# A hybrid decoder block: two gate branches by seven products, earlier long-convolution projections, products issued in a fixed order

## The chip, the cores and the metric

The kernel runs on one core of a Trainium2 chip, in float32. The metric is device time in microseconds (us) of one execution; the number that counts is the median of the runs shown. The engines are TensorE (PE in the rows; PEld is its weight load), VectorE (DVE), ScalarE (ACT), GpSimd (POOL) and SyncE (SP, which issues nearly all weight loads).

## The reference, cut to what matters

512 tokens of width 1024 are normalised and projected; four mixers A to D make branch outputs y of width 256. Each is projected to width 1024 and multiplied by a sigmoid gate; the sum goes through an output projection and an MLP.

```python
D_MODEL, SEQ, N_MIXERS, MIX_W, D_FF = 1024, 512, 4, 256, 4096
xn = _rms(x, norm1_g[l])
# y_a: spatial gate, y_b: sparse attention, y_c: convolution of width 31 and layer norm, y_d: short convolution
z = ca * jax.nn.sigmoid(cb)
z = _causal_depthwise_conv(z, conf_conv_w[l]) + conf_conv_b[l]
y_c = jax.nn.silu(_layernorm(z, conf_ln_g[l], conf_ln_b[l]))
ys = jnp.stack([y_a, y_b, y_c, y_d], axis=2)
proj = jnp.einsum('bsnc,ncd->bsnd', ys, w_branch[l])
gates = jax.nn.sigmoid(jnp.einsum('bsd,de->bse', xn, w_gate[l]) + b_gate[l]).reshape(B, S, N_MIXERS, D)
mixed = jnp.sum(gates * proj, axis=2)
x = x + jnp.einsum('bsd,de->bse', mixed, w_out[l])
hn = _rms(x, norm2_g[l])
hid = jnp.square(jax.nn.relu(jnp.einsum('bsd,df->bsf', hn, w_mlp1[l])))
x = x + jnp.einsum('bsf,fd->bsd', hid, w_mlp2[l])
```

## The kernel before, in words

**Numbers as pairs.** Every float32 operand of a large matmul is held as a hi part and a lo part in a matmul format. ACT makes hi by a cast, DVE makes lo by a subtraction (`split`, L73 to L75). A product of two such operands takes three matmuls: hi with hi, hi with lo, lo with hi (`mm3`, L78 to L81). The transposed xn is XH and XL.

**Stages, in order of PE.** Projections and attention preparation; the gates of branch A (n=0); projections cb, ca, sh, sC, sB of mixers C and D; the gates of branch D (n=3), then B (n=1), then C (n=2); the output projection wo; MLP1 and MLP2 in four rounds (fq). Attention and the long convolution are Tasks: small steps that `tick` puts between the matmuls of the stage that runs. The long convolution's 60 multiply-add steps on DVE (L673) can begin once ca is projected.

**Gates** (`gate_branch`, i the place in that order, n the branch). Output columns go in eight tiles of 128; each is 24 matmuls of 128x512 (8 row blocks by three) into a PSUM tile gt, and a tanh on ACT (L868) into an SBUF tile g. After two gates the piece wb of the branch weights is projected: two tiles pj of 6 matmuls of 128x512. DVE forms (g+1)·pj (L882, L884) and the sum over branches is kept in MIX: written by DVE for the first branch, added to by POOL for the second and third, by DVE for the last (L885), which also splits it into MH and ML for wo.

**Weights** come as a list of pieces in the order of use. `take` hands out the next one; `get` makes two more ahead (ACT cast, DVE subtraction) and starts the loads of two beyond. The hi and lo tiles rotate through 3 buffers each, so the cast for a piece waits until PE has read the piece three before it for the last time.

**Seven products.** From the second part of MLP1 on, a block of 256 output columns by 512 tokens over 1024 rows is cut into quadrants and computed by seven half-size products instead of eight. `Group.make` forms the weight sums on DVE (L189 to L195); the token sums T4 to T7 are made once. `product` issues 24 matmuls of 128x256 per product (L1076 hi·hi, L1079 hi·lo, L1082 lo·hi) into one half of a PSUM tile xz of two banks, product 2 into a tile y of its own. Later products go on adding to what stands in xz; between them ACT copies or DVE adds intermediate values into R, the result in SBUF: after 1 an ACT copy (L1093), after 6 one (L1095), after 7 one (L1099), after 2, 7 and 3 a DVE add (L1089). Product 5 starts in the bank beside 1's, but in the same tile. Names: p27 is product 7 of group 2.

**Order.** The program is emitted in the order above, but a scheduler may reorder PE's work: in MLP1 before the change it put matmuls of other products between two that depend on each other. All dependencies are kept by tile: whoever writes xz waits for the last reader of xz.

Of the kernel before, what the change touches and what calls it, by code (L numbers as in the profile page):

```python
# [8 lines left out]
F32 = mybir.dt.float32  # L9
# [7 lines left out]
P = 128  # L17
# [20 lines left out]
def block_kernel(ctx: ExitStack, tc: tile.TileContext, x, w_in, w_branch, w_gate, w_out,  # L38
# [52 lines left out]
    def piece(name, srcs, nk, alloc=None):  # L91
# [62 lines left out]
    gate_pieces(0)  # L154
    for nm, c in (("cb", C_CB), ("ca", C_CA), ("sh", C_SH), ("sC", C_SC), ("sB", C_SB)):
        win(nm, [(c, 256)], False)
    gate_pieces(3)
    gate_pieces(1)
    gate_pieces(2)
    for q in range(2):  # L160
        for k in range(4):
            piece(f"wo{q}{k}", [w_out[k * 256 : (k + 1) * 256, q * 512 : (q + 1) * 512]], 2,
                  lambda tag, nm: wop[0].tile([P, 1024], F32R, tag=tag, name=f"{tag}_{nm}"))
    NQ = 8
    hps = []
    groups = {}

    class Group:


        def __init__(self, g):
            self.g, self.raw = g, {}

        def load(self):
            if self.raw or not hps:
                return
            for i, j in ((0, 0), (1, 0), (1, 1), (0, 1)):
                r = hps[0].tile([P, 4, 256], F32, tag="rawg", name=f"rawg_{self.g}{i}{j}", bufs=6)
                c0 = (4 * self.g + 2 * i) * P
                nc.sync.dma_start(r, w_mlp1[j * 512 : (j + 1) * 512, c0 : c0 + 256].rearrange("(k p) c -> p k c", p=P))  # L180
                self.raw[i, j] = r

        def make(self, n):
# [3 lines left out]
            if n == 5:  # L187
                self.s = hps[0].tile([P, 4, 256], F32, tag="sg", name=f"sg_{self.g}", bufs=1)
# [8 lines left out]
            v = [walloc(tag, f"p{self.g}{n}")[:, :1024].rearrange("p (k c) -> p k c", k=4) for tag in ("hi", "lo")]  # L197
            split(src, v[0], v[1])
            return v

    seqs = []
    for fq in range(4):
# [14 lines left out]
        for u in seq:  # L217
            if u[0] == "F":
                piece(f"m1_{u[1]}", [w_mlp1[:, u[1] * P : (u[1] + 1) * P]], 8)
            elif u[0] == "P":  # L220
                g = groups.setdefault(u[1], Group(u[1]))
                pieces.append((g.load, lambda g=g, n=u[2]: g.make(n)))
# [627 lines left out]

    MIX = big.tile([P, KT, S], F32, tag="mix", name="MIX")
    MH, ML = [], []

    def gate_branch(i, n, Yf):
        last = i == 3
        Y = None
        for c4 in range(4):
            gts = []
            for j in range(2):
# [7 lines left out]
                gt = br.tile([P, S], F32, tag="gt", name=f"g{n}_{dt}", bufs=4)  # L867
# [29 lines left out]
    gate_branch(0, 0, ya)  # L897

# [8 lines left out]
    def ca_done(j, acc):  # L907
        ca = br.tile([P, S], F32, tag="gt", name=f"ca_{j}", bufs=4)
# [7 lines left out]
    tct = Task(c_tail(), tcv)  # L916

# [37 lines left out]
    np_ = att_stack.enter_context(tc.tile_pool(name="np", bufs=1, side="right", reuse_waits="tile"))  # L955
# [5 lines left out]
    gate_branch(3, 2, yc)  # L961
    assert not tasks

# [97 lines left out]
    xz, yy = {}, {}  # L1061

    def product(g, n, w):
        hi, lo = w
        th, tl = TS[n]
        if n == 1:
            xz[g] = ps2(f"xz_{g}")
            R[g, 0], R[g, 1] = rtile(f"R{g}0"), rtile(f"R{g}1")
        if n == 2:
            yy[g] = ps(f"y_{g}")  # L1070
        acc = yy[g] if n == 2 else xz[g][:, int(n in (3, 5)), :]
        acc = acc.rearrange("p (i c) -> p i c", i=2)
        for p in range(2):
            sl = slice(p * P, (p + 1) * P)
            for kk in range(4):
                nc.tensor.matmul(acc[:, p, :], hi[:, kk, sl], th[:, kk, :],  # L1076
                                 start=kk == 0 and p == 0 and n in (1, 2, 5), stop=False,
                                 skip_group_check=True)
                nc.tensor.matmul(acc[:, p, :], hi[:, kk, sl], tl[:, kk, :], start=False, stop=False,  # L1079
# [133 lines left out]
```

## Time and profile before

| | |
|---|---|
| median of 3 runs | 826.03 us (825.67 to 826.28) |
| the profiled execution | 825.89 us, of which the span is 824.2 us and 1.7 us lie around it |
| PE busy | 806.9 us, 98% of the span |
| DVE busy | 494.3 us, 60% |
| ACT busy | 356.7 us, 43% |
| POOL busy | 86.6 us, 11% |
[...]

The profile prints busy times by engine and by groups of equal instructions, and the idle time before each with the instruction that ended it. Matmuls are pipelined: the printed duration of one (0.39 us for 128x512) is longer than the distance to the next, so the cost of a matmul is read from the distance of two starts.

### The profile page before, as it was taken

How to read it: one execution, taken by the hardware profiler on the slowest of the kernel's cores; microseconds unless marked ns; L12 is line 12 of the kernel's file. 1: busy time of each engine (PE TensorE's matmuls, PEld its weight loads, DVE VectorE, ACT ScalarE, POOL GpSimd, SP SyncE). 2: the span in 40 equal slices, each digit the busy share in tenths (PEclk: the TensorE clock that was granted, in tenths of full speed). 3: DMA queues.
4: the chain of work that ended last, by engine and by line, in shares of the span. 5: the costliest groups of instructions: out<-in, count | busy, mean ns of one | idle time of the engine just before them, and what ended most of it. 6: DMA issues, size and time to landing. Idle time of an engine off the chain costs nothing.

```text
span 824.2 us, 11467 instructions
## 1 busy us (share of the span) xinstructions
PE 806.9 (98%) x4577; PEld 685.9 (83%) x4577; DVE 494.3 (60%) x812; ACT 356.7 (43%) x577; POOL 86.6 (11%) x82
## 2 busy tenths in 40 slices
PE   7999999999999999999999999999999999999998
PEld 5989787777887888888888888889988898889987
DVE  5977764446999635743635758436753575447551
ACT  6645534443433323523524565513662266325630
POOL 6010011122443112120000000000000000000000
PEclk9999999999999999999999999999999999999999
DMA  9272222321222333333454134421442134310121
GB/s 307 82 203 58 74 81 65 103 78 51 65 64 65 115 91 101 90 98 94 143 177 140 39 124 157 128 78 52 119 138 101 30 99 153 104 52 26 52 103 52
DMA packets 94648, 81.41 MB, mean 99 GB/s; under 512 B 3874, under 2 KB 81986, under 8 KB 94595
## 3 DMA queue, kind: packets, MB, share of 16 engines
q1 hardware_dynamic: 93330, 76.61, 30.8%
q10 hardware_dynamic: 720, 2.62, 0.9%
q0 software_dynamic: 544, 1.45, 0.6%
q8 instruction: 36, 0.59, 0.3%
q14 instruction: 18, 0.14, 0.0%
HBM read 78.05 MB, written 2.10 MB: 97 GB/s over the span
## 4 chain that ended last, share of the span: by engine, by line
PE 94%; DVE 2%; ACT 2%; DMA 1%; issue 1%; SPq 1%; DVEq 0%; ACTq 0%
PE gt L79 7%; PE gt L81 7%; PE gt L80 7%; PE o L79 7%; PE o L80 7%; PE o L81 7%; PE xz L1076 5%; PE xz L1082 5%; PE xz L1079 5%; PE pj L79 2%; PE pj L81 2%; PE pj L80 2%; PE wo L81 2%; PE wo L79 2%; PE wo L80 2%; PE pv L605 2%
## 5 line engine op out<-in xcount | busy, mean ns | idle before, releaser
L79 PE MATMUL gt<-XH,hi_wg 128*128 128x512 f32 x256 | 101.8, 398 | 0.0
L81 PE MATMUL gt<-XH,lo_wg 128*128 128x512 f32 x256 | 101.2, 395 | 0.0
L80 PE MATMUL gt<-XL,hi_wg 128*128 128x512 f32 x256 | 100.7, 393 | 0.0
L80 PE MATMUL o<-lo_m,hd 128*128 128x512 f32 x248 | 97.9, 395 | 0.0
L79 PE MATMUL o<-hi_m,hd 128*128 128x512 f32 x248 | 94.5, 395 | 0.0
L81 PE MATMUL o<-hi_m,hd 128*128 128x512 f32 x248 | 93.4, 394 | 0.0
L75 DVE TENSOR_TENSOR lo_wg<-raw_wg,hi_wg 128x1024 fp32r<-128x1024 f32 x32 | 39.1, 1223 | 61.9 <-ACT hi_wg L74 61.8
L75 DVE TENSOR_TENSOR lo_p<-rawg,hi_p 128x1024 fp32r<-128x1024 f32 x35 | 42.8, 1223 | 45.5 <-ACT hi_p L74 45.5
L74 ACT CAST hi_wg<-raw_wg 128x1024 fp32r<-128x1024 f32 x32 | 33.5, 1047 | 82.9 <-PE gt L80 57.9
L74 ACT CAST hi_m<-raw_m 128x1024 fp32r<-128x1024 f32 x36 | 37.7, 1048 | 72.5 <-PE o L81 45.3
L75 DVE TENSOR_TENSOR lo_m<-raw_m,hi_m 128x1024 fp32r<-128x1024 f32 x36 | 44.1, 1224 | 39.0 <-ACT hi_m L74 39.0
L1076 PE MATMUL xz<-T,hi_p 128*128 128x256 f32 x224 | 56.2, 284 | 4.2 <-ACT R L1093 2.2
L583 POOL TENSOR_SCALAR p<-p,c 128x128 f32<-128x128 f32 (+3 forms) x32 | 42.8, 1349 | 157.4 <-DVE c L581 145.5
L81 PEld LDWEIGHTS gt<-XH,lo_wg 128*128 128x128 f32 x256 | 48.1, 188 | 11.8 <-issue 0.5
L74 ACT CAST hi_p<-rawg 128x1024 fp32r<-128x1024 f32 x35 | 36.7, 1049 | 47.1 <-PE xz L1079 23.6
L80 PEld LDWEIGHTS gt<-XL,hi_wg 128*128 128x128 f32 x256 | 48.2, 188 | 10.7
L79 PEld LDWEIGHTS gt<-XH,hi_wg 128*128 128x128 f32 x256 | 48.1, 188 | 10.7 <-issue 0.3
L81 PEld LDWEIGHTS o<-hi_m,hd 128*128 128x128 f32 x248 | 46.6, 188 | 10.9
L1079 PE MATMUL xz<-T,hi_p 128*128 128x256 f32 x224 | 55.6, 281 | 0.0
L80 PEld LDWEIGHTS o<-lo_m,hd 128*128 128x128 f32 x248 | 46.5, 188 | 10.5
L79 PEld LDWEIGHTS o<-hi_m,hd 128*128 128x128 f32 x248 | 46.5, 188 | 10.5
L1076 PEld LDWEIGHTS xz<-T,hi_p 128*128 128x128 f32 x224 | 42.1, 188 | 5.8 <-ACT R L1093 3.1
(405 smaller groups left out, 1870.5 us busy)
## 6 DMA issues: line engine op xcount, KB each, us to landing
raw_m<-in_w_mlp_dram SPq DMA_DIRECT2D x36, 512.0 KB, 3.4
raw_wg<-in_w_gate_dram SPq DMA_DIRECT2D x32, 512.0 KB, 4.0
rawg<-in_w_mlp_dram SPq DMA_DIRECT2D x28, 512.0 KB, 3.7
raw_wb<-in_w_branch_dram SPq DMA_DIRECT2D x16, 256.0 KB, 2.8
raw_wo<-in_w_out_dram SPq DMA_DIRECT2D x8, 512.0 KB, 4.3
x<-in_x_dram SPq DMA_DIRECT2D x4, 512.0 KB, 6.9
raw_kv<-in_w_in_dram SPq DMA_DIRECT2D x4, 512.0 KB, 4.3
w<-in_cmp_w_dram SPq DMA_DIRECT2D x4, 512.0 KB, 6.1
```

Source lines behind the costliest of these rows:

```text
L74: i = nc.scalar.copy(hi, src)
L75: (eng or nc.vector).tensor_tensor(out=lo, in0=src, in1=f32(hi), op=ALU.subtract)
L79: nc.tensor.matmul(dst, l[0], r[0], start=start, stop=False)
L80: nc.tensor.matmul(dst, l[0], r[1], start=False, stop=False)
L81: nc.tensor.matmul(dst, l[1], r[0], start=False, stop=stop)
L583: nc.gpsimd.tensor_scalar_mul(p_[:, b, :w], p_[:, b, :w], c2[:, b : b + 1])
L605: nc.tensor.matmul(dst[i], V[:, k, b, g * HD : (g + 1) * HD], pts[h - 1 + i][:, b, k * P : (k + 1) * P], start=False, stop=b == 1 and k == t)
L1076: nc.tensor.matmul(acc[:, p, :], hi[:, kk, sl], th[:, kk, :], start=kk == 0 and p == 0 and n in (1, 2, 5), stop=False, skip_group_check=True)
L1079: nc.tensor.matmul(acc[:, p, :], hi[:, kk, sl], tl[:, kk, :], start=False, stop=False, skip_group_check=True)
L1082: nc.tensor.matmul(acc[:, p, :], lo[:, kk, sl], th[:, kk, :], start=False, stop=kk == 3 and p == 1 and n in (2, 3, 4), skip_group_check=True)
```

## The change

It does three things. The gates of branches B (n=1) and C (n=2), third and fourth in order, are computed by groups of seven products like MLP1's: two groups per branch, each for 512 gate columns. The hi and lo token sums that this needs (TX4 to TX7) are formed on DVE and ACT from XH and XL after attention has ended, into space that attention's tiles held; TX5 overwrites a quadrant of XH and XL. The pieces cb and ca, and so the long convolution, come before the gates of branch A instead of after them. And each product's matmuls are issued behind the last matmul of the product before (`tc.issue_after`), in MLP1 too.

```diff
+    def seven(g, n, w, TS):
...
+        with tc.issue_after(prod[0].ins) if prod else nullcontext():
...
+        prod[:] = [e]
...
+    def gate_group_pieces(n, first):
+        seq = []
+        for h in range(2):
+            if first and h == 0:
+                o = [1, 2, 5, 6, "J0", 7, "J2", 4, 3]
+            else:
+                o = [1, 5, 6, 2, 7, "J0", 4, 3, "J2"]
...
+    for nm, c in (("cb", C_CB), ("ca", C_CA)):
+        win(nm, [(c, 256)], False)
+    gate_pieces(0)
+    for nm, c in (("sh", C_SH), ("sC", C_SC), ("sB", C_SB)):
+        win(nm, [(c, 256)], False)
+    gate_pieces(3)
+    gate_group_pieces(1, True)
+    gate_group_pieces(2, False)
...
+                acc = seven((n, h), v, w, TX)
...
+                if v == 1:
+                    nc.scalar.copy(r1[:, :, a], acc)
+                elif v == 6:
+                    nc.scalar.copy(r1[:, :, b], acc)
+                elif v == 2:
+                    nc.vector.tensor_tensor(out=r1[:, :, a], in0=r1[:, :, a], in1=acc, op=ALU.add)
+                elif v == 7:
+                    nc.scalar.copy(r2[:, :, b], acc)
+                    nc.vector.tensor_tensor(out=r2[:, :, b], in0=r2[:, :, b], in1=z, op=ALU.add)
+                    for p in range(2):
+                        gate(r2[:, p, b], r2[:, p, b], 4 * h + 2 + p)
+                elif v == 4:
+                    for p in range(2):
+                        gate(r2[:, p, a], acc[:, p, :], 4 * h + 2 + p)
+                elif v == 3:
+                    nc.vector.tensor_tensor(out=r1[:, :, b], in0=r1[:, :, b], in1=z, op=ALU.add)
...
-    gate_branch(2, 1, yb)
+    yb()
     att_stack.close()
...
+    def xdiff(name, a, b):
+        t, u = graw(f"{name}a"), graw(f"{name}b")
+        for d, k in ((t, 0), (u, 1)):
+            nc.vector.tensor_tensor(out=d, in0=f32(a[k]), in1=f32(b[k]), op=ALU.subtract)
+        nc.vector.tensor_tensor(out=t, in0=t, in1=u, op=ALU.add)
+        return t
...
+    t1 = xdiff("tx1", xq[0, 1], xq[0, 0])
+    t3 = xdiff("tx3", xq[1, 1], xq[0, 1])
+    split(t3, *TX[7])
+    t2 = xminus("tx2", xq[1, 1], t1)
+    split(t2, *TX[6])
+    t4_ = xminus("tx4", xq[1, 0], t2)
+    split(t4_, *TX[4])
+    TX[5] = xq[0, 1]
+    split(t1, *TX[5])
+    gate_groups(2, 1, yb)
...
-    gate_branch(3, 2, yc)
+    gate_groups(3, 2, yc)
```

J0 and J2 stand for the two projections of branch weights in a group (pieces wb). In the rows below pg104 is the weight piece of product 4 of branch 1's group 0, pg11... that of its group 1, pm23 that of product 3 of MLP1's group 2; a number at the end of a name is that of a tile. A row with x4 stands for four matmuls.

PE, branch B from product 7 of the first group on. Before, two gates into PSUM tiles of their own, and their projections:

```order
L79 MATMUL gt1_2_3178<-XH_130,hi_wg110_3086 128x512
...
L81 MATMUL gt1_3_3211<-XH_130,lo_wg111_3149 128x512
L79 MATMUL pj1_2_3244<-YB0_140,hi_wb11_3172 128x512
...
L81 MATMUL pj1_3_3253<-YB0_140,lo_wb11_3173 128x512
```

Now:

```order
L916 MATMUL xz_g10_3120<-TX70_3064,lo_pg107_3209 128x256 x4
L81 MATMUL pj1_2_3300<-YB0_140,lo_wb11_3238 128x512
...
L81 MATMUL pj1_3_3307<-YB0_140,lo_wb11_3238 128x512
L911 MATMUL xz_g10_3120<-TX40_3068,hi_pg104_3255 128x256
...
L916 MATMUL xz_g10_3120<-TX40_3068,lo_pg104_3256 128x256 x4
L911 MATMUL xz_g10_3120<-XH_130,hi_pg103_3296 128x256
```

Between products 7 and 4 of this group stand eight matmuls of pj, and product 3 follows product 4 at once.

DVE, the end of the token sums ahead of the first group's product 6 (tx are the sums, sg and rawg the weight sums, crs and csq the layer norm of mixer C, g3 and pj3 the last gates of branch D). Before, at the same projections pj3_6 and pj3_7, DVE has only weight pieces and gates:

```order
L75 TENSOR_TENSOR lo_wg101_3014<-raw_wg101_2947,hi_wg101_3013 128x1024
L884 SCALAR_TENSOR_TENSOR g3_6_2978<-g3_6_2978,pj3_6_3019 128x512
L884 SCALAR_TENSOR_TENSOR g3_7_3011<-g3_7_3011,pj3_7_3028 128x512
L75 TENSOR_TENSOR lo_wb10_3038<-raw_wb10_2984,hi_wb10_3037 128x512
L694 TENSOR_TENSOR cv_2244<-cv_2244,cmu_3068 128x512 x2
```

Now:

```order
L75 TENSOR_TENSOR XL_131<-tx1a_3070,XH_130 128x4x256
L183 TENSOR_TENSOR rawg_g1010_3096<-rawg_g1000_3094,rawg_g1010_3096 128x1024
...
L1025 SCALAR_TENSOR_TENSOR g3_6_3011<-g3_6_3011,pj3_6_3039 128x512
L1025 SCALAR_TENSOR_TENSOR g3_6_3011<-g3_6_3011,pj3_7_3048 128x512
L75 TENSOR_TENSOR TX41_3069<-tx4_3087,TX40_3068 128x1024
L75 TENSOR_TENSOR lo_pg105_3113<-sg_g10_3110,hi_pg105_3112 128x1024
...
L185 TENSOR_TENSOR rawg_g1001_3100<-rawg_g1001_3100,sg_g10_3110 128x1024
L75 TENSOR_TENSOR lo_pg106_3148<-sg_g10_3110,hi_pg106_3147 128x1024
```

Fifteen DVE instructions now stand from the write of XL to the lo part of product 6's weights, the two included.

PE, second round of MLP1. Before, product 5 of the next group and a part of its product 6 stand between products 4 and 3:

```order
L1082 MATMUL xz_3_5146<-HH_3842,lo_p31_5078 128x256 x4
L1076 MATMUL xz_2_4983<-T40_4445,hi_p24_5109 128x256
...
L1082 MATMUL xz_2_4983<-T40_4445,lo_p24_5110 128x256 x4
L1076 MATMUL xz_3_5146<-T50_4430,hi_p35_5176 128x256
...
L1076 MATMUL xz_3_5146<-T60_4440,hi_p36_5207 128x256
L1076 MATMUL xz_2_4983<-HH_3842,hi_p23_5142 128x256
```

Now product 3 follows product 4:

```order
L916 MATMUL xz_m3_5545<-HH_4239,lo_pm31_5475 128x256 x4
L911 MATMUL xz_m2_5382<-T40_4842,hi_pm24_5506 128x256
...
L916 MATMUL xz_m2_5382<-T40_4842,lo_pm24_5507 128x256 x4
L911 MATMUL xz_m2_5382<-HH_4239,hi_pm23_5539 128x256
...
L916 MATMUL xz_m2_5382<-HH_4239,lo_pm23_5540 128x256 x4
L911 MATMUL xz_m3_5545<-T50_4827,hi_pm35_5573 128x256
```

The same holds in the third and fourth rounds.

## Rows read from the trace of the kernel before

**Rows 1.** The page: busy time by engine, and the granted clock in 40 slices.

```profile
PE 806.9 (98%) x4577; PEld 685.9 (83%) x4577; DVE 494.3 (60%) x812; ACT 356.7 (43%) x577; POOL 86.6 (11%) x82
...
PEclk9999999999999999999999999999999999999999
```

**Rows 2.** Waits of PE: who waited, for whom, us in total, times, longest.

```profile
PE xz L1076 <- ACT R L1093: 2.2, 4, 0.7
PE xz L1076 <- DVE R L1089: 1.9, 3, 0.6
PE xz L1076 <- ACT hi_p L74: 1.6, 1, 1.6
PE xz L1076 <- ACT R L1053: 1.2, 1, 1.2
PE y L1082 <- DVE lo_p L75: 0.8, 1, 0.8
```

**Rows 3.** Timeline of PE, one gate: start, duration, instruction, [idle before <-releaser].

```profile
354.76 0.40 PE L79 MATMUL gt<-XH,hi_wg 128*128 128x512 f32 x1
...
362.88 0.39 PE L81 MATMUL gt<-XH,lo_wg 128*128 128x512 f32 x1
```

**Rows 4.** Timeline of PE, product 1 and the start of product 5 in MLP1.

```profile
562.05 0.28 PE L1076 MATMUL xz<-HH,hi_p 128*128 128x256 f32 x1
...
563.47 0.29 PE L1076 MATMUL xz<-HH,hi_p 128*128 128x256 f32 x1
...
564.42 0.63 PE L1082 MATMUL xz<-HH,lo_p 128*128 128x256 f32 x4
565.73 0.38 PE L1076 MATMUL xz<-T,hi_p 128*128 128x256 f32 x1 [0.67 <-ACT R L1093]
565.96 0.28 PE L1079 MATMUL xz<-T,hi_p 128*128 128x256 f32 x1
```

**Rows 5.** Timeline of PE, ACT and DVE, product 7 to product 4 in MLP1.

```profile
577.67 0.63 PE L1082 MATMUL xz<-T,lo_p 128*128 128x256 f32 x4
577.87 1.05 ACT L74 CAST hi_p<-rawg 128x1024 fp32r<-128x1024 f32 x1 [0.56 <-PE xz L1079]
...
578.83 0.58 ACT L1099 COPY R<-xz 128x512 f32<-128x512 f32 x1
...
580.10 0.68 DVE L1089 TENSOR_TENSOR R<-R,xz 128x512 f32<-128x512 f32 x1
...
580.83 0.38 PE L1076 MATMUL xz<-T,hi_p 128*128 128x256 f32 x1 [0.65 <-DVE R L1089]
```

**Rows 6.** Timeline of PE, the first MLP1 group: product 3 behind product 4.

```profile
525.76 0.38 PE L1076 MATMUL xz<-HH,hi_p 128*128 128x256 f32 x1 [1.17 <-ACT R L1053]
```

**Rows 7.** Timeline, the first MLP1 group: product 2's wait, behind half of product 5.

```profile
498.91 0.38 PE L1076 MATMUL xz<-T,hi_p 128*128 128x256 f32 x1 [0.22 <-ACT R L1093]
...
499.84 0.27 PE L1079 MATMUL xz<-T,hi_p 128*128 128x256 f32 x1
...
500.88 0.74 PE L1082 MATMUL y<-HH,lo_p 128*128 128x256 f32 x4 [0.77 <-DVE lo_p L75]
```

**Rows 8.** Groups of DVE and POOL instructions: busy us, mean ns | idle before.

```profile
L673 DVE SCALAR_TENSOR_TENSOR cv<-Z,sm,cv 128x512 f32<-128x512 f32 x60 | 45.6, 790 | 0.4
...
L75 DVE TENSOR_TENSOR lo_wg<-raw_wg,hi_wg 128x1024 fp32r<-128x1024 f32 x32 | 39.1, 1223 | 61.9 <-ACT hi_wg L74 61.8
...
L884 DVE SCALAR_TENSOR_TENSOR g<-g,pj 128x512 f32<-128x512 f32 x24 | 16.3, 683 | 7.7 <-PE pj L81 7.5
```

**Rows 9.** Timeline of DVE around two adds of POOL to MIX.

```profile
264.95 0.68 DVE L884 SCALAR_TENSOR_TENSOR g<-g,pj 128x512 f32<-128x512 f32 x1
265.55 1.19 DVE L75 TENSOR_TENSOR lo_wb<-raw_wb,hi_wb 128x512 fp32r<-128x512 f32 x1
266.65 1.78 DVE L673 SCALAR_TENSOR_TENSOR cv<-Z,sm,cv 128x512 f32<-128x512 f32 x1
```

**Rows 10.** Timeline of PE and ACT: a cast for the next branch weights, waiting.

```profile
351.51 0.39 PE L80 MATMUL pj<-YB,hi_wb 128*128 128x512 f32 x1
351.94 0.62 ACT L74 CAST hi_wb<-raw_wb 128x512 fp32r<-128x512 f32 x1 [1.09 <-PE pj L80]
```

**Rows 11.** Busy us (instructions) by stretch of PE, PEld, DVE, ACT, POOL; clock, DMA share, GB/s.

```profile
205.00:240.00 35.00, 35.00 (x175) 28.10 (x174) 35.00 (x54) 14.21 (x26) 13.89 (x7) 1.00 0.22 62
240.00:268.00 28.00, 28.00 (x153) 22.21 (x152) 26.85 (x39) 9.76 (x17) 11.66 (x6) 1.00 0.22 66
```

More of the change, by code (lines that the diff above doesn't have):

```diff
@@ L849, in block_kernel @@
         proj_T("gu", gu_done, j)
+    xz, yy, prod = {}, {}, []
+    def seven(g, n, w, TS):
+        hi, lo = w
+        th, tl = TS[n]
+        if n == 1:
+            xz[g] = ps2(f"xz_{groups[g].name}")
+        if n == 2:
+            yy[g] = ps(f"y_{groups[g].name}")
+        acc = yy[g] if n == 2 else xz[g][:, int(n in (3, 5)), :]
+        acc = acc.rearrange("p (i c) -> p i c", i=2)
+        with tc.issue_after(prod[0].ins) if prod else nullcontext():
+            for p in range(2):
+                sl = slice(p * P, (p + 1) * P)
+                for kk in range(4):
+                    nc.tensor.matmul(acc[:, p, :], hi[:, kk, sl], th[:, kk, :],
+                                     start=kk == 0 and p == 0 and n in (1, 2, 5), stop=False, skip_group_check=True)
+                    nc.tensor.matmul(acc[:, p, :], hi[:, kk, sl], tl[:, kk, :], start=False, stop=False,
+                                     skip_group_check=True)
+                for kk in range(4):
+                    e = nc.tensor.matmul(acc[:, p, :], lo[:, kk, sl], th[:, kk, :], start=False,
+                                         stop=kk == 3 and p == 1 and n in (2, 3, 4), skip_group_check=True)
+        prod[:] = [e]
+        for _ in range(2):
+            tick()
+        return acc
@@ L851, in block_kernel, with branch_mm, mix_in @@
     MIX = big.tile([P, KT, S], F32, tag="mix", name="MIX")
     MH, ML = [], []
+    def branch_mm(n, c4, Y):
+        w, = take()
+        r = []
+        for j in range(2):
+            dt = 2 * c4 + j
+            pp = ps(f"pj{n}_{dt}")
+            sl = slice(j * P, (j + 1) * P)
+            for c in range(2):
+                mm3(pp, (w[0][:, c, sl], w[1][:, c, sl]), (Y[0][:, c, :], Y[1][:, c, :]), c == 0, c == 1)
+            r.append((dt, pp))
+        return r
+    def mix_in(i, dt, gt, pp):
+        mx = MIX[:, dt, :]
+        last = i == 3
+        nc.vector.scalar_tensor_tensor(out=gt, in0=gt, scalar=1.0, in1=pp, op0=ALU.add, op1=ALU.mult)
+        (nc.vector if last else nc.gpsimd).tensor_tensor(out=mx, in0=mx, in1=gt, op=ALU.add)
+        if last:
+            if dt % 2 == 0:
+                MH.append(t4(f"MH{dt}", [P, 2, S], F32R))
+                ML.append(t4(f"ML{dt}", [P, 2, S], F32R))
+            split(mx, MH[-1][:, dt % 2, :], ML[-1][:, dt % 2, :])
```

138 lines of the change are left out of this document (91 added, 47 removed).

## Prediction

> **What bounds the kernel now.** I read the busy times by engine first: PE is busy 98% of the span at the full granted clock, DVE 60%, ACT 43% [rows 1]. So the kernel is worth what PE's instruction stream is worth, plus PE's waits. The list of PE's waits comes second: behind the start, all that is longer than half a microsecond lies in MLP1's seven-product part, about 7.7 us together [rows 2]; in the stages that the change rebuilds PE waits for nothing. Third, the timelines give prices. A change can therefore win only by taking columns off PE, and loses by every wait that it brings into a stage that has none.
>
> **The price of a matmul.** Of a gate, 36 starts lie between 354.76 and 362.88: 8.12 / 35 = 0.232 us per 128x512 matmul [rows 3]. Of a product, 12 matmuls lie between 562.05 and 563.47: 0.1183 us per 128x256, so 24 of them cost 2.84 us [rows 4].
>
> **The price of a wait.** At product 5 behind product 1 the trace prints 0.67 us of idle time. The last matmul of product 1 has its slot until 564.42 + 4 x 0.118 = 564.90, so PE lost 0.83 up to 565.73, and the first matmul after it takes 0.23 instead of 0.12 [rows 4]. One such wait costs 0.94 us. The printed 1.17 of product 3 directly behind product 4 [rows 6] costs 0.50 more, 1.44.
>
> **Columns saved.** Each group replaces four gates, 96 x 0.232 = 22.27 us, by seven products, 168 x 0.1183 = 19.87 us. Four groups: 9.6 us less PE work. The branch projections stay the same.
>
> **Waits inside the groups.** The same dependencies by tile that give the waits of MLP1 come with the products. I take them by pair, with 0.94 as the lower price and about 1.9 as the upper one (0.94 and one ACT cast of 1.05 [rows 5] that stands ahead of the copy in ACT's queue).
>
> 1 to 5: in three groups product 5 directly follows product 1, and waits for ACT's copy out of the same xz tile. In groups 1 of B and 0 of C a weight cast and, in the first, a tanh stand ahead of that copy on ACT; I take 1.4, 1.6 and 0.94: 3.9 (2.8 to 5.7). The first group puts product 2 between, which covers it.
>
> 7 to 4: product 4 waits for the DVE add that follows ACT's copy. In MLP1 product 7's last slot ended at 577.67 + 4 x 0.118 = 578.14, the add at 580.78, and product 4 started at 580.83: 2.69 us behind [rows 5]. The groups of the second order have more than 2.8 us of other matmuls there, so nothing is lost. The first group has only eight pj matmuls, 8 x 0.232 = 1.86: 0.83 + 0.11 = 0.94 lost, and DVE has a backlog there; I take 1.5 (0.9 to 1.9).
>
> 4 to 3: product 3 waits for ACT's reading of 4's result. The second order puts eight pj matmuls between, so none; the first group has none between, and two tanh instructions and a cast have to pass on ACT: nearest is the row with 1.17; I take 1.75 (0.9 to 1.9).
>
> Second branch weights J2: with three buffers the hi cast of a group's second wb waits until PE has read the first one's last hi part, and PE's next instruction but one wants it. In the row, the cast starts 0.43 after the start of that matmul and takes 0.62 [rows 10]; PE has two matmuls, 0.46, to do until then, so about 0.6 + 0.11 = 0.7 is lost, in three groups: 2.1 (0 if the casts are released earlier, to 2.4).
>
> **First group's token sums.** They begin when attention's tiles are free. The place that decides is XL's quadrant: its ACT cast (1.05, and 0.3 of release) waits for branch D's last gate, then DVE has to pass fifteen instructions to the lo part of product 6: eight of 1024 columns and seven of 512. By the durations of 1.22 and 0.68 and the overlap of 0.08 between neighbours [rows 8, 9] that is 8 x 1.14 + 7 x 0.60 = 13.3 us, in all 14.7. PE has meanwhile 12 + 4 projection matmuls, three products and 8 matmuls of the fourth: 16 x 0.232 + 80 x 0.1183 = 13.2 us. So PE waits 1.5 us (0, if the casts come earlier, to 2.3, if all earlier sums are late too).
>
> What the row says of POOL beside this: DVE's instructions with both inputs in SBUF took 1.19 and 1.78 us while POOL added to MIX, against some 0.68 and 0.79 for their size [rows 8], and the one with an input in PSUM kept its 0.68 [rows 9]. [...]
>
> Sum of waits in the groups: 3.9 + 1.5 + 1.75 + 2.1 + 1.5 = 10.8 us (4.6 to 14.2). Against 9.6 saved: **+1.2 us** (-5.0 to +4.6).
>
> **Long convolution moved ahead of branch A's gates.** It adds no instruction. Its 60 steps of about 0.67 to 0.79 us [rows 8] leave a stretch where DVE is full: 35.0 of 35 us and 26.9 of 28, PE waiting for nothing [rows 11]. In the new place, from ca's projection to A's last one, I add up 72 us of DVE work against 280 matmuls of 128x512 and the small ones of attention, some 75 us of PE. DVE is nearly full there, in small steps between the lo parts of the weights, and those are made two pieces ahead. The rows show that PE gets through such a stretch, so I cost it at nothing; without that cover it costs what DVE exceeds PE by. The eight matmuls of its layer norm only move from branch B to branch D.
>
> **Fixed order in MLP1.** First group: half of product 5 ran while product 2's lo part was late, and PE still waited 0.77 [rows 7]. Without that filler (8 matmuls, 0.95 us) the wait is 0.95 longer. Rounds two to four: the wait of product 4 for DVE (0.65 each, three times [rows 2]; 0.9 with the restart) goes, since all 24 matmuls of the next product 1 (2.84) now stand before it and the add needs 2.69. In its place product 3 directly follows product 4 and waits for ACT: 0.94 each. Net zero; the three waits of 1 to 5 stay. In all **+0.95 us** (-1.8, if ACT is early at 4 to 3, to +2.5, if it costs 1.44 each).
>
> **Forecast.** 825.89 + 1.2 + 0.95 = 828.0 in the profiled execution; that run lies 0.14 below the median, so 828.2 us. About 0.2% is what a measurement of this kernel tells from no change: the bounds are 824.4 and 827.7, so this is slower, by little.
>
> **Rivals.** *The waits are as small as in MLP1's own groups.* There a round of 14 products shows two waits, 0.67 and 0.65 [rows 2], so 0.94 per group. Four groups: 3.8, no wait for sums or branch weights. Then 9.6 - 3.8 = 5.8 saved, MLP1 gives 0.95 back: 821.2 us, faster. For it: same code, same engines, and the copies' queues on ACT are only half full (43%). Against it: MLP1 runs two groups into each other, so that one covers the other's pairs, and the gates don't. It decides where the waits in the groups sum to less than 7.0 us. *The waits eat the saving exactly*: a wait sum of 7.0 to 10.3, 824.4 to 827.7, middle 826. *DVE's backlog reaches PE.* Where conv, softmax steps and lo parts share DVE, POOL's work stretches two-input steps by 0.5 to 1.1 us [rows 9]; ten such steps more than I counted turn 72 us of DVE into 80 against 75 of PE, and 5 us of wait come on top of 828: about 833. For it speaks DVE at 100% [rows 11], against it that PE didn't wait there before. [...] *That the change doesn't do what it says* I give nothing: the order shows seven products per group and no mixing.
>
> **How the numbers follow.** Forecast, slower by 0.3 to 5 us: 0.36; DVE backlog, above that: 0.11; even: 0.24; small waits, faster: 0.29. The range reaches from the small-waits case, 821.2, to near the backlog case, 832.5; beyond it I leave some 0.1 at either end. The forecast's own range is 827.7 to 831. Chances: faster 0.29, within 0.2% 0.24, slower 0.47.
>
> **What the changed profile should show.** PE busy time less by about 9 us, but waits of 11 us more. In PE's list of waits: three of product 5 for the ACT copy in the groups, one each of products 4 and 3 in the first group, of product 6 for its weights or sums, three of pj for hi_wb; in MLP1 three of product 3 for ACT and none of product 4 for DVE; product 2's at 1.7 us. From ca to the end of A's gates no wait. Between the first product of B and the first matmul of wo 1.2 us more than before between B's first gate and wo (488 x 0.232 = 113 us). The prediction is wrong if this list is short (the waits were overrated) or if waits for lo_wg appear beside the convolution.

## The result: slower by 1.45%, and the profile after

The changed kernel takes 838.05 us in the median of 4 runs (836.38 to 839.07); the kernel before took 825.85 us beside it (825.52 to 826.28). The ratio is 1.0145, with a 95% interval of 1.0128 to 1.0163. The sign was forecast, but the size was not: 828.2 us was forecast, with a range up to 832.5.

The profiled execution has a span of 837.3 us, 13.1 more than before. First come the lines of the profile's page that answer to [rows 1]:

```profile
PE 804.8 (96%) x4865; PEld 699.1 (83%) x4865; DVE 554.2 (66%) x866; ACT 379.8 (45%) x613; POOL 88.0 (11%) x82
...
PE   7999999999999998898999998999999999999998
```

Compared with 806.9, PE's busy time falls by 2.1 us, where the prediction wanted about 9 and the four groups hold 9.6 us less work by starts; DVE has 60 us more. The stages, by the starts of their first matmuls:

| stage | before, us | after, us | difference |
|---|---|---|---|
| up to the first product of B (before: first gate) | 308.35 | 310.13 | +1.8 |
| B and C, up to wo | 113.2 | 121.0 | +7.8 |
| wo | 45.7 | 45.7 | 0 |
| MLP1, first tiles | 26.7 | 27.5 | +0.8 |
| MLP1's products and MLP2, to PE's last product of MLP1 | 293.2 | 295.9 | +2.8 |

The 1.8 us of the first row are the eight layer norm matmuls (8 x 0.232) that moved there from the second one. So B and C lost 9.6 us where 1.2 were forecast, and the seven-product part of MLP1 lost 2.8 where 0.95 was forecast. The 0.8 us in MLP1's first tiles were not forecast at all: PE waits 1.09 us there for the lo part of the normalised tokens, HL, instead of 0.20. In every profile with branch C in groups this wait is 0.66 to 1.61 us, and in those without groups it is 0.20; why HL comes later was not followed.

PE's waits of the whole kernel (who waited, for whom, us in total, times, longest), which answer to [rows 2]:

```profile
PE xz_g L911 <- ACT g L970: 5.8, 3, 3.6
PE xz_m L911 <- ACT R L1227: 3.2, 4, 1.2
...
PE xz_g L916 <- DVE lo_pg L75: 2.2, 1, 2.2
PE xz_m L911 <- ACT R L1248: 2.0, 3, 0.7
PE y_m L916 <- DVE lo_pm L75: 2.0, 1, 2.0
...
PE xz_g L911 <- ACT g L955: 1.4, 1, 1.4
PE pj L79 <- ACT hi_wb L74: 1.4, 3, 0.5
PE y_g L916 <- DVE lo_pg L75: 1.2, 1, 1.2
PE xz_g L911 <- DVE g L977: 1.2, 1, 1.2
```

The list has the entries that the prediction named: product 5 for ACT's copy three times (5.8 us), product 4 for DVE (1.2) and product 3 for ACT's tanh (1.4) in the first group, three waits for projection weights (1.4), product 2 of MLP1 (2.0), and in MLP1 product 3 for ACT (0.7 each) with no wait of product 4 for DVE left. Two things are not as written: the first of these is 3.6 us long in one place, and the first group waits for the lo parts of products 2 (1.2) and 5 (2.2), ahead of product 6, while product 6 itself waits only 0.18.

A part of the rest is in the granted clock. Stretches of PE alone (us, PE busy and number of instructions, granted clock, DMA share, GB/s):

```profile
320.50:324.00 3.50, 3.32 (x17) 0.59 0.27 87
...
379.00:383.00 4.00, 3.90 (x20) 0.57 0.00 0
...
511.50:516.00 4.50, 4.50 (x25) 0.62 0.19 47
```

Each stretch stands right behind one of the three longest waits (the start of the kernel aside). The row PEclk on the page does not show them: each lasts some 3 of the 21 us of a slice, and all 40 slices still read 9. Timeline of PE (start, duration, instruction, idle before):

```profile
320.50 0.74 PE L916 MATMUL xz_g<-XH,lo_pg 128*128 128x256 f32 x4 [2.16 <-DVE lo_pg L75]
...
379.10 0.57 PE L911 MATMUL xz_g<-XH,hi_pg 128*128 128x256 f32 x1 [3.62 <-ACT g L970]
...
380.11 0.41 PE L911 MATMUL xz_g<-XH,hi_pg 128*128 128x256 f32 x1
380.32 0.41 PE L913 MATMUL xz_g<-XL,hi_pg 128*128 128x256 f32 x1
...
511.46 0.74 PE L916 MATMUL y_m<-HH,lo_pm 128*128 128x256 f32 x4 [2.00 <-DVE lo_pm L75]
```

At 380.11 the starts lie 0.21 us apart instead of 0.118. Inside each of the three stretches the granted clock reads 0.50 (322 to 324, 380 to 382 and 513 to 515 us), ahead of it and behind it 1.00. Product 5 of C's first group takes 383.57 - 379.10 = 4.47 us instead of 2.84. In this execution the clock falls behind the waits of 2.16, 3.62 and 2.00 us; behind those of up to 1.62 us it stays at 1.00.

**Why the first group waits.** DVE, beside the last gates of D and the first products:

```profile
281.94 1.21 DVE L1105 TENSOR_TENSOR tx1a<-XH 128x1024 f32<-128x1024 f32 x1
...
288.02 2.32 DVE L1106 TENSOR_TENSOR tx1a<-tx1a,tx1b 128x1024 f32<-128x1024 f32 x1
...
294.26 3.34 DVE L747 RECIPROCAL crs<-csq 128x512 f32<-128x512 f32 x1
...
303.39 1.78 DVE L75 TENSOR_TENSOR lo_wb<-raw_wb,hi_wb 128x512 fp32r<-128x512 f32 x1
...
311.37 1.21 DVE L75 TENSOR_TENSOR XL<-tx1a,XH 128x1024 fp32r<-128x1024 f32 x1
...
316.31 1.93 DVE L75 TENSOR_TENSOR TX<-tx,TX 128x1024 fp32r<-128x1024 f32 x1
318.16 2.28 DVE L75 TENSOR_TENSOR lo_pg<-sg_g,hi_pg 128x1024 fp32r<-128x1024 f32 x1
```

POOL in the same stretch:

```profile
301.62 3.00 POOL L1026 TENSOR_TENSOR MIX<-MIX,g 128x512 f32<-128x512 f32 x2 [12.37 <-DVE g L1025]
315.86 3.50 POOL L1026 TENSOR_TENSOR MIX<-MIX,g 128x512 f32<-128x512 f32 x2 [11.24 <-DVE g L1025]
```

How full the engines were (us, then busy us of PE, PEld, DVE, ACT, POOL, clock, DMA share, GB/s):

```profile
290.00:300.00 10.00, 10.00 (x45) 8.10 (x44) 10.00 (x9) 6.45 (x8) 0.00 (x0) 1.00 0.29 87
300.00:310.00 10.00, 10.00 (x45) 8.12 (x44) 10.00 (x10) 5.22 (x6) 3.00 (x2) 1.00 0.93 298
310.00:320.00 10.00, 7.14 (x58) 6.69 (x56) 10.00 (x10) 2.49 (x3) 3.50 (x2) 1.00 0.27 78
```

From the first token sum on DVE never rests. XL's quadrant, which the prediction took as the place that decides, could have been written at 305.8, when its ACT cast had ended; DVE came to it at 311.37. And five instructions with two SBUF inputs beside POOL's work (it adds from 287.57 to 289.25, too) take 1.4 to 2.3 us where others of their size take 0.68 or 1.21.

**Why C's first group waits 3.62 us.** ACT, DVE and POOL ahead of 379.10:

```profile
370.66 3.52 POOL L942 TENSOR_TENSOR MIX<-MIX,g 128x512 f32<-128x512 f32 x2 [18.82 <-DVE g L941]
...
371.03 2.00 DVE L75 TENSOR_TENSOR lo_pg<-sg_g,hi_pg 128x1024 fp32r<-128x1024 f32 x1
373.06 2.19 DVE L181 TENSOR_TENSOR sg_g<-sg_g,rawg_g 128x1024 f32<-128x1024 f32 x1
...
375.35 1.04 ACT L74 CAST hi_pg<-sg_g 128x1024 fp32r<-128x1024 f32 x1 [4.65 <-DVE sg_g L181]
376.30 1.33 ACT L955 ACTIVATE g<-g,hb 128x512 f32<-128x512 f32 x2
377.54 1.03 ACT L74 CAST hi_pg<-rawg_g 128x1024 fp32r<-128x1024 f32 x1
378.47 0.57 ACT L970 COPY g<-xz_g 128x512 f32<-128x512 f32 x1
```

Read from the bottom: the copy out of product 1's result, which product 5 waits for, stands in ACT's queue behind a cast, two tanh and a second cast. The first cast, of the weight sum sg, starts after 4.65 us of idle time, when DVE has made sg, and that sum and the lo part before it take 2.19 and 2.00 us beside POOL's adds to MIX; without these adds they take 1.23 and 1.22 (the run with POOL's adds left out, below). Product 1 had ended at 375.3.

### The profile page after: what moved, and what is told of

Read it like the earlier page. It is cut to its first block, busy times and chain, and to the rows that moved or that the text cites. A ratio compares the mean times of both kernels' runs of the same rounds, so it can differ in the third digit from the quotient of the medians.

```text
span 837.3 us, 12137 instructions
## 1 busy us (share of the span) xinstructions
PE 804.8 (96%) x4865; PEld 699.1 (83%) x4865; DVE 554.2 (66%) x866; ACT 379.8 (45%) x613; POOL 88.0 (11%) x82
## 3 DMA queue, kind: packets, MB, share of 16 engines
q0 software_dynamic: 544, 1.45, 0.6%
## 4 chain that ended last, share of the span: by engine, by line
PE 84%; DVE 7%; ACT 3%; issue 3%; DMA 2%; SPq 0%; DVEq 0%; ACTq 0%
PE o L79 7%; PE o L80 7%; PE o L81 7%; PE xz_m L911 5%; PE xz_m L913 5%; PE xz_m L916 5%; PE gt L79 3%; PE gt L81 3%; PE gt L80 3%; PE xz_g L911 2%; PE xz_g L913 2%; PE xz_g L916 2%; PE pj L79 2%; PE pv L650 1%; PE pj L80 1%
## 5 line engine op out<-in xcount | busy, mean ns | idle before, releaser
L75 DVE TENSOR_TENSOR lo_pm<-rawg_m,hi_pm 128x1024 fp32r<-128x1024 f32 x35 | 42.7, 1221 | 38.8 <-ACT hi_pm L74 38.8
L911 PE MATMUL xz_m<-T,hi_pm 128*128 128x256 f32 x224 | 56.4, 284 | 2.0 <-ACT R L1248 2.0
L74 ACT CAST hi_pm<-rawg_m 128x1024 fp32r<-128x1024 f32 x35 | 36.8, 1050 | 46.3 <-PE o L81 20.6
L913 PE MATMUL xz_m<-T,hi_pm 128*128 128x256 f32 x224 | 55.9, 282 | 0.0
L81 PEld LDWEIGHTS o<-hi_m,hd 128*128 128x128 f32 x248 | 46.6, 188 | 10.8
L79 PE MATMUL gt<-XH,hi_wg 128*128 128x512 f32 x128 | 51.5, 403 | 0.0
L81 PE MATMUL gt<-XH,lo_wg 128*128 128x512 f32 x128 | 50.6, 396 | 0.0
L80 PE MATMUL gt<-XL,hi_wg 128*128 128x512 f32 x128 | 50.6, 395 | 0.0
L1298 DVE TENSOR_TENSOR X<-X,o 128x512 f32<-128x512 f32 x31 | 21.3, 687 | 39.6 <-PE o L81 39.6
L911 PEld LDWEIGHTS xz_m<-T,hi_pm 128*128 128x128 f32 x224 | 42.6, 190 | 3.0 <-ACT R L1248 2.6
L718 DVE SCALAR_TENSOR_TENSOR cv<-Z,sm,cv 128x512 f32<-128x512 f32 x60 | 43.8, 761 | 0.2
L913 PEld LDWEIGHTS xz_m<-T,hi_pm 128*128 128x128 f32 x224 | 42.5, 190 | 0.4
L916 PE MATMUL xz_m<-T,lo_pm 128*128 128x256 f32 x224 | 35.6, 281 | 0.0
```

The costliest lines, as they stand in the source:

```text
L74: i = nc.scalar.copy(hi, src)
L75: (eng or nc.vector).tensor_tensor(out=lo, in0=src, in1=f32(hi), op=ALU.subtract)
L79: nc.tensor.matmul(dst, l[0], r[0], start=start, stop=False)
L80: nc.tensor.matmul(dst, l[0], r[1], start=False, stop=False)
L81: nc.tensor.matmul(dst, l[1], r[0], start=False, stop=stop)
L718: nc.vector.scalar_tensor_tensor(out=cv[:, j, :], in0=Z[:, j, k : k + S], scalar=wc, in1=cv[:, j, :], op0=ALU.mult, op1=ALU.add)
```

## The experiments

All runs were timed beside the kernel before; the ratio is to it.

### The three parts of the change, one at a time

**The fixed order, undone in the changed kernel:**

```diff
-        with tc.issue_after(prod[0].ins) if prod else nullcontext():
+        with nullcontext():
```

> The changed kernel, with the scheduler again free to put other matmuls between products, in the gates and in MLP1. If the groups' waits for ACT and DVE are the cause (theory), the pairs 1 to 5 get half of product 2 and the pair 4 to 3 the next product 1 between them, worth some 2 us of printed waits, but the first group's waits for lo parts (1.19 and 2.16 us) and the 3.62 us before product 5 of C's first group stand on DVE's and ACT's queues and mostly stay: 832 to 836 us. If the fixed order is the cause (rival), 825 to 828 us.

Measured: 836.83 us (ratio 1.0133, 1.011 to 1.0156), just above the expected range and far from the rival. PE's waits:

```profile
PE y_g L911 <- ACT hi_pg L74: 6.7, 3, 3.1
...
PE xz_g L916 <- DVE lo_pg L75: 2.4, 2, 2.2
```

The scheduler put half of product 2 before product 5, and now PE stands at product 2, for a hi part that ACT has not cast: 2.44 and 3.08 us at the same places as before, with the lower clock behind both (0.68 from 348 to 352, 0.74 from 376 to 380). In MLP1 the wait for product 2's lo part falls from 2.00 to 0.54. The free order is no cure in the groups, so the fixed one is not what makes them wait.

**The convolution, put back in the changed kernel** (its projections and their pieces again behind branch A's gates).

> The changed kernel, with the projections cb and ca and the long convolution back behind branch A's gates. Theory: the layer norm of mixer C (a reciprocal of 3.35 us and some ten smaller instructions, about 8 us of DVE) no longer stands ahead of the first group's token sums, so the waits of 1.19 and 2.16 us and the half clock behind them go, 4 to 5 us; but the same work then lies among the groups of B: 833 to 836 us. Rival, that the move of the convolution costs the time: 826 to 828 us. Rival, that the place of the convolution plays no part: 838 us.

Measured: 836.70 us (1.0125, 1.0108 to 1.0143), 0.7 above the expected range. The first group's waits for lo parts have gone altogether, as the theory said. In their place, with the layer norm now among B's groups:

```profile
PE xz_g L911 <- ACT g L970: 6.6, 3, 3.6
...
PE xz_g L911 <- DVE g L977: 2.3, 1, 2.3
```

Product 4 of the first group waits 2.3 us instead of 1.2, product 5 of the second 2.25 instead of 1.50, each with the lower clock behind it (0.64 from 332 to 336, 0.72 from 348 to 352). All the waits in B and C together fall from 13.4 to 11.8 us, and the time by 1.35, within the spread of the two kernels' runs (834.3 to 837.7 and 836.4 to 839.1): most of what the first group gains, the later ones lose.

**The fixed order alone, in the kernel before:**

```diff
-        for p in range(2):
+        with tc.issue_after(prod[0].ins) if prod else nullcontext():
+            for p in range(2):
...
+        prod[:] = [e]
```

> The kernel before, with the products of MLP1 in fixed order and nothing else. Theory: product 2 of the first group waits some 1.2 us longer, and in rounds two to four the wait moves from product 4 to product 3, from 0.65 to 1.0 us each: 826.8 to 828.5 us. Rival, that the gates' fixed order alone costs: 825.9 us, no change.

Measured: 828.08 us (1.0025, 1.0015 to 1.0035), within the expectation. The waits of MLP1 are those of the changed kernel:

```profile
PE xz L1077 <- ACT R L1053: 3.2, 4, 1.2
...
PE y L1083 <- DVE lo_p L75: 2.0, 1, 2.0
```

The single runs lie in two heaps, 827.3 to 827.6 and 828.6 to 829.0. The profiled execution is of the lower heap and has the full clock behind the 2.0 us (1.00 from 500 to 510); the changed kernel's profile has the lower clock there (0.62 from 511.5 to 516) and 1.6 us more in this stage. So the fixed order costs 1.2 us (294.4 against 293.2 from the first product to the last), and in some executions the clock takes as much again. Further profiles with this order in MLP1 agree: three with the lower clock behind this wait take 295.7 to 295.9 us for the stage (the changed kernel, and below the runs without POOL's adds and with product 2 early), three without it 294.2 to 294.4 (this run, the convolution put back, and the filled waits below). That the upper heap here is the lower clock is likely by this, but none of its executions was profiled.

**The convolution alone, in the kernel before.**

> The kernel before, with cb, ca and the long convolution ahead of branch A's gates and nothing else. Theory: nothing, 825.4 to 826.4 us, since PE shows no wait between ca and D's gates in the changed kernel. Rival, that DVE's full stretch reaches PE: 828 to 833 us.

Measured: 825.21 us (0.9991, 0.9981 to 1.0000). PE waits for nothing in the new place. The median is 0.9 us lower, with an interval that reaches no change; in the profiled execution 0.7 of that is a shorter wait before the first transposes (2.2 against 2.9 us), a wait that lies anywhere from 2.2 to 3.0 in the profiles of this case. So a gain from the move itself is not shown.

By difference, if the three parts add up, the groups with their fixed order thus cost some 11 us of the 12.2.

### What makes the waits

**POOL's adds left out** (the terms of branch D's last two tiles and all of branch B are missing from the sum):

```diff
-        (nc.vector if last else nc.gpsimd).tensor_tensor(out=mx, in0=mx, in1=gt, op=ALU.add)
         if last:
+            nc.vector.tensor_tensor(out=mx, in0=mx, in1=gt, op=ALU.add)
```

> The changed kernel without POOL's adds to MIX after branch D's last two projections and in all of branch B (left out, so the sum over branches misses those terms). Theory: DVE's instructions with two SBUF inputs keep 1.2 us instead of 1.9 to 2.3 beside the first group and C's first group; the 2.16 us before the first product 5 shrinks to under 1, the 3.62 us before C's product 5 to about 2, and with them at least one of the two stretches at the lower clock goes: 831 to 834 us. Rival, that the order of the queues on DVE and ACT alone makes the waits: 837 to 838 us.

Measured: 834.37 us (1.0088, 1.0067 to 1.0109), 3.7 us less than the changed kernel and just above the expected range. PE at the two places, and the two DVE instructions that took 1.93 and 2.28 us:

```profile
316.55 1.21 DVE L75 TENSOR_TENSOR TX<-tx,TX 128x1024 fp32r<-128x1024 f32 x1
317.69 1.21 DVE L75 TENSOR_TENSOR lo_pg<-sg_g,hi_pg 128x1024 fp32r<-128x1024 f32 x1
318.95 0.74 PE L916 MATMUL xz_g<-XH,lo_pg 128*128 128x256 f32 x4 [0.36 <-DVE lo_pg L75]
322.42 0.39 PE L911 MATMUL xz_g<-TX,hi_pg 128*128 128x256 f32 x1 [1.31 <-ACT hi_pg L74]
...
375.50 0.39 PE L911 MATMUL xz_g<-XH,hi_pg 128*128 128x256 f32 x1 [1.87 <-ACT g L971]
```

2.16 became 0.36, and 3.62 became 1.87, as expected. But 1.31 came up at product 6, which hides part of the first. These adds of POOL beside DVE are about a third of the loss (three of the stretched instructions, before 305 us, keep theirs); that the order of the queues makes the rest is not shown by this run.

**Product 2 before product 5 in all groups:**

```diff
-                o = [1, 5, 6, 2, 7, "J0", 4, 3, "J2"]
+                o = [1, 2, 5, 6, 7, "J0", 4, 3, "J2"]
```

> The changed kernel with product 2 between products 1 and 5 in all four groups. Theory: ACT's copy of product 1's result then stands ahead of the cast for product 6, which waits for DVE's weight sum, and product 2 covers it; the waits of 1.50, 3.62 and 0.73 us go with the half clock behind the second: 829 to 832 us. Rival, that PE then waits at product 6 or 2 for weights instead, because DVE is late in any case: 835 to 838 us.

Measured: 835.05 us (1.0109, 1.009 to 1.0127), outside the theory's range and at the lower edge of the rival's. The waits 1 to 5 have gone, so the theory's mechanism holds. But the second projection, which in the changed kernel had come to stand between products 4 and 3, was no longer issued there, and two more groups now wait between 4 and 3 (1.40 and 1.39 us, beside the first group's 1.44 as before).

**The same, with MLP1 free for the scheduler.**

> As the run with product 2 early, and MLP1's products free for the scheduler again, the gates' ones fixed. Theory: the 2.0 us that the fixed order cost alone come off: 827 to 830 us. Rival, that the fixed order in MLP1 costs nothing once the stages ahead are disturbed: as the run before, within 0.5 us.

Measured: 832.77 us (1.0082, 1.0067 to 1.0097), 2.3 us less: the 2.0 us of the fixed order again. The time is above the expected range, as the run before was above its own. This pair tells of the clock, too. Both profiles wait 1.2 and then 2.1 or 2.2 us at the same places of the first group, and then for product 6 (0.64 and 1.31); one execution has the lower clock behind it (first line), the other has not in the whole stage (second line; the columns as above, for B and C):

```profile
309.80:428.60 118.80, 107.75 (x770) 0.97 0.31 95
```

```profile
309.80:427.30 117.50, 105.17 (x769) 1.00 0.31 96
```

The first line's execution takes 1.3 us longer, although its waits add up to less (11.0 against 12.3 us). Behind a wait of 2.16 us at the first group's product 5 the clock fell in the changed kernel's profile, and did not fall here: it differs from one execution to the next.

**The two longest waits filled** with 30 matmuls each, whose result nothing uses:

```diff
                 acc = seven((n, h), v, w, TX)
+                if (n, h, v) in ((1, 0, 2), (2, 0, 1)):
+                    dz = ps("dz")
+                    with tc.issue_after(prod[0].ins):
+                        for q in range(30):
+                            e = nc.tensor.matmul(dz[:, 0:256], TX[1][0][:, q % 4, 0:128], TX[1][0][:, q % 4, :],
+                                                 start=q == 0, stop=q == 29, skip_group_check=True)
+                    prod[:] = [e]
```

> The changed kernel with 30 matmuls of 128x256 (3.5 us) more at two places, their result unused: ahead of product 5 of B's first group, and behind product 1 of C's first group, where PE waited 2.16 and 3.62 us and the lower clock followed. Theory: they lie in the waits, the clock stays at its upper level there, and the 1.7 to 1.9 us that each stretch at the lower clock cost come off: 833.5 to 836 us. Rival, that the lower clock is no cost of its own: 838 us or, where the filler is longer than the wait, up to 841 us.

Measured: 836.33 us (1.0133, 1.0116 to 1.0151), 1.7 us less than the changed kernel with 60 matmuls more, between the theory's range and the rival's. The single runs spread from 835.2 to 838.3, those of the changed kernel from 836.4 to 839.1, so that it is faster as a whole is not shown. The clock in the two places:

```profile
316.80:325.00 8.20, 8.03 (x66) 1.00 0.38 108
374.90:383.00 8.10, 8.06 (x68) 1.00 0.01 2
```

From the first product of B to wo the profiled execution took 119.5 us instead of 121.0. This gain belongs to the second place: in the first, product 6 starts 13.8 to 13.9 us behind the first product in either kernel, since it waits for DVE's chain, and the lower clock was hidden behind that. In these two executions a stretch at the lower clock cost about 1.5 us where PE was not late in any case, and little where it was.

### Versions without the causes

**Branch C alone by groups**: B by plain gates, and the token sums formed beside them, so that only TX5 is written after B's last gate; product 2 early, MLP1 free.

> Only branch C by seven products, with product 2 early and MLP1 free; branch B by plain gates, and the token sums formed beside them (only the write of the quadrant of XH and XL waits for B's last gate). Theory: 4.8 us of columns saved, some 1.5 to 3 us of short waits left (projection weights, 7 to 4, 4 to 3), the convolution's 0.9 us kept, no lower clock: 821 to 824 us. Rival, that DVE, with weight sums, lo parts and the last branch's MIX work, is the bound of C's groups whatever lies ahead: 826 us or more.

Measured: 824.62 us (0.9983, 0.9973 to 0.9992), above the expectation by half a microsecond. No group waits for a lo part or a sum: with a plain branch beside it DVE's chain is covered. What is left is 1.40 between 4 and 3 and 0.9 us in smaller waits, and behind the groups 1.12 for HL.

**The same, with one projection held between 7 and 4 and the other between 4 and 3:**

```diff
-                o = [1, 2, 5, 6, 7, "J0", 4, 3, "J2"]
+                o = [1, 2, 5, 6, 7, "J0", 4, "J2", 3]
...
-                waiting += branch_mm(n, v, Y)
+                with tc.issue_after(prod[0].ins):
+                    waiting += branch_mm(n, v, Y)
```

> As the run with branch C alone by seven products, and now both projections of a group are held in place too: one between products 7 and 4, the other between 4 and 3, 12 matmuls (2.78 us) each. Theory: the 1.40 us between 4 and 3 and the waits for projection weights (0.23, 0.47) go, some 2.5 to 3 us with the restarts: 821.5 to 823 us. Rival, that DVE or ACT are late in C's groups in any case and the waits move to other products: 824.6 us, no change.

Measured: 824.63 us (0.9983, 0.9973 to 0.9992): no change from the run before, so the expectation failed. All waits that it was to remove have gone, and two others have come, at product 7, which waits for ACT's copy out of product 6's result:

```profile
378.05 0.39 PE L911 MATMUL xz_g<-TX,hi_pg 128*128 128x256 f32 x1 [1.15 <-ACT g L973]
...
405.20 0.38 PE L911 MATMUL xz_g<-TX,hi_pg 128*128 128x256 f32 x1 [1.44 <-ACT g L973]
```

Before, a projection had stood there by chance. A group has four pairs that depend on each other (1 to 5, 6 to 7, 7 to 4, 4 to 3) and three fillers; I had counted three pairs.

The profiled execution is the longest of the ten (826.40 us), and shows the lower clock from 467 to 471 us (0.67 from 468 to 472), behind a wait of no more than 1.33 us, with 0.24 us just ahead of it:

```profile
467.02 0.41 PE L80 MATMUL h<-HL,hi_m 128*128 128x256 f32 x1 [1.33 <-DVE HL L75]
```

So the 2.0 us seen above are no lower bound for such a fall.

**The second half of B by a group too**, with the sums beside its first half.

> As the run before, and the second half of branch B by a group too; the token sums have B's first half, some 28 us of PE, beside them. Theory: another 2.4 us of columns saved, if the sums and weight sums keep up: 819.5 to 821.5 us. Rival, that the first group after the sums waits for DVE as in the changed kernel: 823 us or more.

Measured: 824.06 us (0.9976, 0.9967 to 0.9986). Another 2.4 us of columns gave 0.6 in the median, less than the intervals tell apart: the new group brings its own wait of 1.15 at product 7, and C's first group one of 0.36 at product 4. The time lies in the rival's range, but no group waits for the sums, so its mechanism is not what was seen.

**Both branches by groups, with those fillers.**

> Both branches by groups as in the changed kernel, product 2 early, the projections held between 7 and 4 and between 4 and 3, MLP1 free. Theory: all waits between products of a group go, some 11 us with their restarts, one stretch at the lower clock and MLP1's 2.0 us; what stays is the first group's lateness of DVE, 1.2, 2.2 and 1.3 us, at times with the lower clock behind it: 823 to 827 us. Rival, that DVE is late through all four groups: 830 us or more.

Measured: 830.87 us (1.0066, 1.005 to 1.0082): the rival's time, but not its mechanism, since DVE is late in the first group alone. Product 7 waits 1.15 to 1.41 us in three groups, and the first group is late as it was, for 1.19, 2.16, 1.30 and 1.13 us in a row, with a clock of 0.50 from 325 to 335 us; this execution is the longest of the four (833.55 us).

**A filler for every pair**: in the version with half of B, the projections are held by halves of 6 matmuls, one between 6 and 7, two between 7 and 4, one between 4 and 3.

```diff
+        for kind, h, v in seq:
+            if kind == "J":
+                if late:
+                    out.append(late)
+                out.append(("J", h, (v, 0)))
+                late = ("J", h, (v, 1))
+            else:
+                if v == 3:
+                    out.append(late)
+                    late = None
+                out.append((kind, h, v))
```

> The second half of B and all of C by groups, product 2 early, and the projections held in halves: one tile pj (6 matmuls, 1.39 us) between products 6 and 7, two between 7 and 4, one between 4 and 3. The runs before had only three fillers for four pairs that depend on each other, and one pair (6 to 7, or 4 to 3) always waited 1.15 to 1.45 us. Theory: those waits go, 3 x 1.4 to 1.7 us with the restarts: 819.5 to 821.5 us. Rival, that ACT and DVE, not the pairs, set the pace of a group, so that the wait turns up at weights: 823.5 to 824.5 us.

Measured: 821.85 us (0.9955, 0.9940 to 0.9970), just above the expected range and the fastest of all, 4 us below the kernel before and 16 below the changed one. In its three groups PE waits once, and for the reason that was met above, a copy behind a cast that waits, here for a load:

```profile
377.19 1.04 ACT L74 CAST hi_wo<-raw_wo 128x1024 fp32r<-128x1024 f32 x1 [2.12 <-DMA raw_wo<-in_w_out_dram]
378.14 0.58 ACT L992 COPY g<-xz_g 128x512 f32<-128x512 f32 x1
...
378.77 0.38 PE L925 MATMUL xz_g<-TX,hi_pg 128*128 128x256 f32 x1 [2.49 <-ACT g L992]
```

The clock stays at 1.00 behind these 2.49 us. Without the wait some 2.5 us more would be had, by estimate; that was not tried.

## Why the prediction was wrong, point by point

**Prices and saved columns: right.** The groups' matmuls start 0.118 us apart at the full clock, the plain gates' 0.232 [rows 3, 4]. That the waits decide whether the saving is kept was right, and so was the sign; the clock, below, was a second term.

**The pairs: three of four terms right.** 7 to 4: 1.5 priced, 1.18 idle and 0.27 of restart measured. 4 to 3: 1.75 priced, 1.45 and 0.27 measured. Projection weights: 2.1 priced, three of 0.47 and their restarts measured. 1 to 5 was priced at 3.9; its three waits were 1.50, 3.62 and 0.73, with restarts 6.7. The step that failed is the 1.6 us for C's first group, where 3.62 and the restart make 3.9: I counted the casts that stand ahead of the copy on ACT at their own duration, but the first of them waited 4.65 us for a DVE sum. ACT's queue passed on the waits of what stood ahead, and not only its durations. The runs without POOL's adds (1.87) and with product 2 early (none) show both halves of that.

**The first group's sums: mis-sized, 1.5 us for about 5.** This is the other step that failed. The prediction let the last fifteen DVE instructions begin with XL's release by the last gate. DVE was already behind: its whole chain from the end of attention on runs without a break, five of its instructions stretched beside POOL, by 0.7 to 1.1 us each (4.7 in all). Product 6 started 13.8 us behind the first product, where the three products between take 8.5; so PE lost 5.3 there, whichever of it was idle time, restart or lower clock. The runs with the layer norm or the sums elsewhere (the convolution put back; branch C alone) have none of its waits for lo parts. Beside POOL's adds four of DVE's instructions with two SBUF inputs took 2.00, 2.19, 1.93 and 2.28 us, against 1.21 to 1.23 for the same four in the run without those adds: 3.5 us together. The prediction had such a stretch in a row [rows 9] (POOL's two adds run there from 264.57 to 267.88 us) and gave it no term in its sum. The 0.3 of release in that sum was my estimate; in the changed kernel the cast starts 0.43 us after the start of the gate's matmul that it waits for (304.32 to 304.75), 0.04 after its printed end.

**The clock: left out.** No term of the sum held it. Three stretches at the lower clock, 0.50, stand in the profiled execution; by the runs above one is worth about 1.5 us in C's first group, about as much in MLP1, and little in the first group. That it differs by execution fits the spread of the changed kernel's runs: 836.38 us with a mean granted clock of 0.997, 837.95 with 0.995, and 838.14 and 839.07 with 0.993.

**MLP1: right without the clock.** 0.95 priced, 1.2 measured by the fixed order alone, and the wait moved from product 4 to product 3 as written; about 1.5 us more came from the clock (295.7 to 295.9 against 294.2 to 294.4 in six profiles).

**The convolution: right alone, not together.** It was costed at nothing, and alone it costs nothing (825.21 us). In the changed kernel its layer norm, with a reciprocal of 3.34 us, stands in DVE's chain ahead of the first group; with the convolution put back, the first group's waits for lo parts are gone.

**The rivals.** The backlog of DVE, at 833 us, came nearest: its mechanism, two-input steps stretched beside POOL, was at work, but not in the convolution's stage, where I had put it, and at a higher price. The small waits would have needed a filler for every pair. *MLP1's first tiles*, 0.8 us, were in no term of the sum.

The sum, after the fact: 13.4 us of idle time in the groups, 3.0 for eleven restarts of 0.27, 2.8 at the lower clock (1.5 in C's first group, 1.3 in B's, which there only takes the place of idle time) make 19.2, less 9.6 saved: 9.6, as measured. The restart of 0.27 and the clock's 1.5 and 1.3 are estimates, from rows of this trace. Of the excess of 8.4 over the 10.8 forecast, about 4.3 lie at the pairs 1 to 5, nearly all at C's first group with its clock, and about 4.1 at the first group with its own. The sign was right, but on too small a sum of waits: 10.8 were priced, and 19.2 came.

## What to carry to other kernels

Before a stage without waits is rebuilt from steps that depend on each other, count the pairs and give each its own filler: a filler moved from one pair uncovers another, and three fillers moved about among four pairs gained nothing (824.62 and 824.63 us). On an engine that works in the order of its queue, price what stands ahead of the awaited instruction by when its inputs arrive, not by its duration (here a cast of 1.04 us that had waited 4.65 us); start such a chain at the point from which the engine never rests. And where PE would wait for some two microseconds, add the lower clock behind the wait to the upper end of its price (it followed 13 of the 19 waits of 1.87 us and more here, and cost some 1.5 us by estimate), unless PE is late there in any case.

## What the runs showed of the hardware that I had not expected

The granted clock fell, from 1.00 to 0.50, behind single idle times of a PE that was otherwise busy for hundreds of microseconds, and not always. Of the 19 idle times of 1.87 us and more in the fifteen profiles (the start of the kernel aside), 13 have the lower clock right behind them, 1.87 to 3.62 us long, and six have not, 2.0 to 2.49 us long. It fell once behind 1.33 us, where it stayed at 1.00 behind 1.32 us in another run (both branches with the fillers held), and once only in the course of a row of four waits (2.16, then 1.30 and 1.13 us). It came back within 3 to 10 us. Filling such a wait with matmuls that nothing uses kept the clock at 1.00 in both places; whether this makes the kernel faster is open, with 836.33 against 838.05 us and runs that overlap.
